# Attention scores of the latent tokens as three float32r products of split operands

## The chip, the cores and the metric

The kernel runs on one core of a Trainium2 chip. The metric is the device time of one execution in microseconds (us); lower is better. TensorE (PE) multiplies, VectorE (DVE) and ScalarE (ACT) do elementwise work and reductions, GpSimd (POOL) and SyncE (SP) mostly issue transfers. Each engine works through its own queue in order and waits at an instruction whose inputs are not there.

## The reference, cut to what matters

One inference step of a two-layer backbone (DEPTH 2) with D_MODEL 1024: 128 context tokens and 256 latent tokens pass through the same weights. A layer is a half-step feed-forward block, a mixer (short convolution, neighbourhood attention NA, latent attention MLA, three gates), and a second feed-forward block. The change touches the scores of both attentions, which have 8 heads each:

```python
# NA: latent queries against the latent keys of the grid (biased, masked) and the cached context keys
s_loc = jnp.einsum('bhrqd,bhrikd->bhrqik', qg, kg).astype(jnp.float32) * NA_SCALE + bias[None]
...
s_ctx = jnp.einsum('bhrqd,bhpd->bhrqp', qg, k_ctx).astype(jnp.float32) * NA_SCALE
prob = jax.nn.softmax(jnp.concatenate([s_loc, s_ctx], axis=-1), axis=-1).astype(v.dtype)
# MLA: latent queries against 256 latent and 128 cached keys; context queries against context keys
s = jnp.einsum('bhqd,bhkd->bhqk', qi, k).astype(jnp.float32) * scale
p = jax.nn.softmax(s, axis=-1).astype(v.dtype)
```

## The kernel before

All 384 tokens lie along the free axis; features lie on partitions. Every dense weight is streamed from memory in chunks of 128x1024 ("raw"), split on chip into a rounded part and a remainder in float32r ("hi" by ScalarE in line 318, "lo" by VectorE in line 319), and multiplied by activations that are split in the same way: three float32r matmuls for each 128-row block (lines 360 to 362, helper mm3). A dense tile is 8 blocks, so 24 matmuls. The attention values and scores are native float32 matmuls on unsplit operands.

The instructions stand in each queue in the order in which the program writes them (a manual schedule). The mixer's function attention works through the MLA heads 0 to 7 one at a time and then through the NA heads in pairs (8,9), (10,11), (12,13), (14,15). For an MLA head i the loop writes: scores([i]); mla_query(i + 2), which makes a later head's query (VectorE, line 945) and, for even heads, the keys of two heads (two ScalarE copies, lines 950 and 951); FILL[i] dense tiles of the convolution branch, each 24 matmuls, with its VectorE work in lines 822 to 838; for odd i the product values(i - 3) of probabilities and values; and transposed(i - 1), seven TensorE transposes of the previous head's probabilities. FILL is 1 behind heads 0, 1, 2, 4 and 6, and 0 behind heads 3, 5 and 7.

scores itself issues the matmuls (lines 862 and 864: two latent query tiles of 128x384, and the context queries of 128x128), then the softmax: three maxima on VectorE (line 877, for NA line 873 with the bias added), a small scaling (line 878), three exponentials on ScalarE (line 883), a reciprocal and three scalings on VectorE (lines 885 and 890). An NA head has 64 features, so two heads of a pair sit on partitions 0 to 63 and 64 to 127 of one tile, and their matmuls use the two halves of the array's rows (the trace writes 64\*128).

Eight PSUM banks (tile ps) rotate through all of this, and eight SBUF tiles of 128x384 (tile w) through all temporaries.

Of the kernel before, what the change touches and what calls it, by code (L numbers as in the profile page):

```python
# [10 lines left out]
F32R = mybir.dt.float32r  # L11
# [7 lines left out]
P = 128  # L19
# [5 lines left out]
NCTX = 128  # L25
NLAT = 256
TOK = NCTX + NLAT
PAST = 128
# [245 lines left out]
class Weights:  # L274
# [49 lines left out]
    def prepare(self):  # L324

        self.split(self.n // BPC + self.ahead)
# [16 lines left out]
def step_kernel(ctx, tc, xT, cc, wst, cst_d, vec_d, rpb, ck_na, cv_na, ck_kv, ck_r, yd, o_k, o_v, o_ckv, o_kr):  # L343
    nc = tc.nc
# [4 lines left out]
    def ps():  # L349
        return psum.tile([P, 512], F32, tag="ps", name="ps")  # L350

    def wt(n=TOK):
        return base.tile([P, TOK], F32, tag="w", bufs=8, name="w")[:, :n]

    def small(n, dtype=F32):
        return base.tile([P, 16], dtype, tag="small", bufs=16, name="small")[:, :n]

    def mm3(out, w, x, start, stop):

        nc.tensor.matmul(out, w[0], x[0], start=start, stop=False)  # L360
        nc.tensor.matmul(out, w[0], x[1], start=False, stop=False)  # L361
        nc.tensor.matmul(out, w[1], x[0], start=False, stop=stop)  # L362

    def split(hi, lo, full):
        nc.scalar.copy(hi, full)  # L365
        nc.vector.tensor_tensor(lo, full, hi.bitcast(F32), op=ALU.subtract)  # L366
# [217 lines left out]
    def dense_tile(h, n=KD, halfway=None):  # L584

        out = ps()
        for k in range(n):
            if halfway and k == n // 2:
                halfway()
            mm3(out[:, :TOK], W.next(), kt(h, k), k == 0, k == n - 1)  # L590
        return out
# [81 lines left out]
    def mixers(l):  # L673
# [6 lines left out]
        with tc.tile_pool(name=f"att{l}", bufs=1, reuse_waits="tile") as pool:  # L680
            attention(l, h, pool, o_conv, o_na, o_mla)
# [33 lines left out]
    def attention(l, h, pool, o_conv, o_na, o_mla):  # L715

        kna = pool.tile([P, 4, ALLK], F32, tag="A8", bufs=3, name="kna")
        qna = pool.tile([P, 4, TOK], F32, name="qna")
# [9 lines left out]
        def bias(heads):  # L728

            for hd in heads:  # L730
                t = biases[hd] = pool.tile([P, 2, TOK], F32, tag="C3", bufs=2, name="bias")
                nc.gpsimd.memset(t[:, :, NLAT:], 0.0)
                nc.gpsimd.dma_start(out=t[:, :, 0:NLAT], in_=rpb[l, hd])
            for hd in heads:
                for qt in range(2):
                    d = biases[hd][:, qt, 0:NLAT].rearrange("p (r c) -> p r c", r=4)
                    nc.gpsimd.tensor_tensor(d, d, cst[:, C_MASK:C_END].unsqueeze(1).to_broadcast([P, 4, 64]),
                                            op=ALU.add)


        low, rb, b = first_group(l, 1)
# [3 lines left out]
        qs, q2, ks = wt(), wt(), wt()  # L745
# [96 lines left out]

        probs, probsT, queries, mla, na = {}, {}, {}, {}, {}

        def scores(heads):


            near = heads[0] >= 8
            scale = 1.0 if near else MLA_SCALE
            operands, tiles = [], []  # L850
            for i in heads:
                if near:
                    r, j = slice(64 * (i % 2), 64 * (i % 2) + 64), i % 8 // 2
                    operands.append((qna[r, j, :], kna[r, j, :]))
                else:
                    operands.append((queries.pop(i), mla["k"][:, i % 4, :]))
                s = ps(), ps()
                tiles.append((s[0][:, :TOK], s[1][:, :TOK], s[0][:, TOK:]))
            for j in range(3):
                for (q, k), s in zip(operands, tiles):  # L860
                    if j < 2:
                        nc.tensor.matmul(s[j], q[:, NCTX + j * P:NCTX + (j + 1) * P], k[:, NCTX:], start=True, stop=True)  # L862
                    else:
                        nc.tensor.matmul(s[2], q[:, :NCTX], k[:, :NCTX], start=True, stop=True)
            cols = [slice(0, TOK), slice(TOK, 2 * TOK), slice(2 * TOK, 2 * TOK + NCTX)]
            n = 3 * len(heads)
            mx, nm, sm, rs = small(n), small(n), small(n), small(n)
            for a, (i, s) in enumerate(zip(heads, tiles)):
                probs[i] = pool.tile([P, 2 * TOK + NCTX], F32, tag="prob", bufs=2, name="prob")
                for j in range(3):  # L870
                    m = mx[:, 3 * a + j:3 * a + j + 1]
                    if near and j < 2:
                        nc.vector.tensor_tensor_reduce(
                            out=probs[i][:, cols[j]], in0=s[j], in1=biases[i % 8][:, j, :], scale=1.0, scalar=-3.0e38,
                            op0=ALU.add, op1=ALU.max, accum_out=m)
                    else:
                        nc.vector.tensor_reduce(m, s[j], axis=AX.X, op=ALU.max)
            nc.vector.tensor_scalar(nm, mx, -scale, None, op0=ALU.mult)
            for a, (i, s) in enumerate(zip(heads, tiles)):
                for j in range(3):  # L880
                    c = 3 * a + j
                    src = probs[i][:, cols[j]] if near and j < 2 else s[j]
                    nc.scalar.activation(probs[i][:, cols[j]], src, AF.Exp, bias=nm[:, c:c + 1], scale=scale,
                                         accum_out=sm[:, c:c + 1])
            nc.vector.reciprocal(rs, sm)
            for a, i in enumerate(heads):
                for j in range(3):
                    c = 3 * a + j
                    p = probs[i][:, cols[j]]
                    nc.vector.tensor_scalar(p, p, rs[:, c:c + 1], None, op0=ALU.mult)  # L890
                biases.pop(i - 8, None)
# [29 lines left out]
        def mla_values():  # L921
            v = mla["v"] = pool.tile([P, 4, 512], F32, tag="A8", bufs=3, name="vmla")
            wh, wl = W.next(4)
            for i in range(4):
                o = ps()
                xh, xl = ckh[:, i * P:(i + 1) * P], ckl[:, i * P:(i + 1) * P]
                nc.tensor.matmul(o, xh, wh, start=True, stop=False)
                nc.tensor.matmul(o, xl, wh, start=False, stop=False)
                nc.tensor.matmul(o, xh, wl, start=False, stop=True)
                (nc.scalar.copy if i % 2 else nc.vector.tensor_copy)(v[:, i, :], o)  # L930

        def mla_query(hd):


            if hd == 0:
                k = mla["k"] = pool.tile([P, 4, ALLK], F32, tag="A8", bufs=3, name="kmla")

                kr = ps()
                nc.tensor.matmul(kr, cst[0:64, C_PM:C_MASK], R, start=True, stop=True)
                nc.scalar.copy(k[0:64, 0::2, :], kr[0:64, :].unsqueeze(1).to_broadcast([64, 2, ALLK]))  # L940
                nc.scalar.copy(k[64:128, 1::2, :], kr[64:128, :].unsqueeze(1).to_broadcast([64, 2, ALLK]))
            o = dense_tile((cqh, cql), 2)
            q = pool.tile([P, TOK], F32, tag="qmla", bufs=3, name="qmla")
            cs = cst[:, C_CSO:C_CSK] if hd % 2 else cst[:, C_CSE:C_CSO]
            nc.vector.tensor_tensor(q, o[:, :TOK], cs, op=ALU.mult)
            queries[hd] = q
            if hd % 2 == 0:
                o = ps()
                mm3(o, W.next(), (ckh, ckl), True, True)
                nc.scalar.copy(mla["k"][64:128, hd % 4, :], o[64:128, :])  # L950
                nc.scalar.copy(mla["k"][0:64, hd % 4 + 1, :], o[0:64, :])

        mla_values()
        mla_query(0)
        mla_query(1)
        for i in range(8):
            scores([i])
            if i + 2 < 8:
                mla_query(i + 2)
            if i == 6:  # L960
                bias([0, 1])
            for _ in range(FILL[i]):
                next(conv)
            if i >= 3 and i % 2:
                values(i - 3)
            if i >= 1:
                transposed(i - 1)
        for i in range(8, 18, 2):
            if i > 8:
                transposed(i - 2)  # L970
                transposed(i - 1)
            if i < 16:
                scores([i, i + 1])
                if i < 14:
                    bias([i - 6, i - 5])
            if i == 8:
                transposed(7)
                na_values()
            for _ in range(FILL[i]):
                next(conv)  # L980
            values(i - 2)
# [64 lines left out]
```

## Time and profile before

| what | value |
|---|---|
| time, median of 3 runs | 1907.8 us (1905.85 to 1907.82) |
| time of the profiled execution | 1906.98 us |
| its span, first to last instruction | 1904.9 us |
| TensorE matmul busy | 1878.2 us, 99% |
| TensorE weight loads busy | 1822.4 us, 96% |
| VectorE busy | 1309.2 us, 69% |
| ScalarE busy | 808.2 us, 42% |
| mean granted TensorE clock | 0.997 of 2.4 GHz |
| heads' scores of layer 0, on TensorE | from 372.9 us; the last of MLA's 8 heads starts at 421.2 us |

Between the span and the time of the execution lie 2.1 us. Matmuls are pipelined: the record of one lasts longer than the distance to the next, so a matmul's price is read from start to start. A native float32 matmul shows as two records, so "x4" in a row of line 862 is two matmuls.

### The profile page before, as it was taken

The numbers are of one execution on the slowest core, as the hardware profiler recorded it, in microseconds if no ns is written. First come the engines' busy times: TensorE is split into PE (matmuls) and PEld (weight loads), VectorE is DVE, ScalarE is ACT, GpSimd is POOL, SyncE is SP. The second block draws the span as 40 slices with busy tenths as digits, with TensorE's granted clock in tenths as the row PEclk, the third lists the DMA queues.
The fourth block names the chain that finished last, engine by engine and source line by source line (L and its number), as shares of the span: only waits on it lengthen the run. The fifth ranks groups of instructions, "written<-read, shape, count | busy, mean of one in ns | idle before, by whom it ended". The sixth has DMA issues, their size and how long they took to land.

```text
span 1904.9 us, 27714 instructions
## 1 busy us (share of the span) xinstructions
PE 1878.2 (99%) x10804; PEld 1822.4 (96%) x10804; DVE 1309.2 (69%) x2235; ACT 808.2 (42%) x1358; POOL 45.0 (2%) x79
## 2 busy tenths in 40 slices
PE   7999999999999999999999999999999999999998
PEld 5999999988999999999999999998789999999998
DVE  6788767665877778776678777676668766744433
ACT  3633334755533454333354333356554334633332
POOL 0000000013000000000000000000220000000000
PEclk9999999999999999999999999999999999999999
DMA  8576655323465535665545665543335543333331
GB/s 305 188 241 223 192 182 162 122 78 112 135 196 184 181 111 188 193 199 190 171 135 191 195 208 180 170 134 118 100 100 176 192 163 122 114 131 123 131 122 67
DMA packets 85523, 306.12 MB, mean 161 GB/s; under 512 B 9616, under 2 KB 11248, under 8 KB 85264
## 3 DMA queue, kind: packets, MB, share of 16 engines
q1 hardware_dynamic: 83376, 297.21, 47.5%
q0 software_dynamic: 1728, 5.41, 1.0%
q8 instruction: 84, 1.38, 0.3%
q10 hardware_dynamic: 288, 1.74, 0.2%
q14 instruction: 47, 0.39, 0.1%
HBM read 301.53 MB, written 2.79 MB: 160 GB/s over the span
## 4 chain that ended last, share of the span: by engine, by line
PE 87%; DVE 6%; ACT 4%; issue 2%; DMA 1%; SPq 0%; DVEq 0%; ACTq 0%
PE ps L361 27%; PE ps L362 27%; PE ps L360 27%; ACT w L525 2%; PE ps L862 1%; PE ps L899 1%; ACT hi L318 1%; DMA raw<-wst 1%; PE ps L915 1%; DVE lo L319 1%; PE ps L808 1%; PE ps L806 1%; PE ps L807 1%; DVE w L433 1%; DVE w L434 1%
## 5 line engine op out<-in xcount | busy, mean ns | idle before, releaser
L361 PE MATMUL ps<-hl,hi 128*128 128x384 f32 (+1 forms) x2176 | 738.4, 339 | 3.1 <-DVE hl L366 2.1
L360 PE MATMUL ps<-hh,hi 128*128 128x384 f32 (+1 forms) x2176 | 735.0, 338 | 3.0 <-ACT hh L365 1.5
L362 PE MATMUL ps<-hh,lo 128*128 128x384 f32 (+1 forms) x2176 | 737.3, 339 | 0.5 <-DVE lo L319 0.5
L319 DVE TENSOR_TENSOR lo<-raw,hi 128x1024 fp32r<-128x1024 f32 x414 | 503.6, 1223 | 226.6 <-ACT hi L318 225.2
L318 ACT CAST hi<-raw 128x1024 fp32r<-128x1024 f32 x414 | 431.0, 1047 | 410.8 <-PE ps L361 268.3
L360 PEld LDWEIGHTS ps<-hh,hi 128*128 128x128 f32 x2176 | 411.1, 189 | 8.4 <-ACT hh L365 4.2
L361 PEld LDWEIGHTS ps<-hl,hi 128*128 128x128 f32 x2176 | 409.6, 188 | 7.0 <-DVE hl L366 5.2
L362 PEld LDWEIGHTS ps<-hh,lo 128*128 128x128 f32 x2176 | 411.3, 189 | 0.9 <-DVE lo L319 0.9
L422 DVE SCALAR_TENSOR_TENSOR junk<-rawa,cb 128x1024 bf16<-128x1024 f32 x256 | 312.8, 1222 | 4.4
L360 PE MATMUL ps<-ah,hi 128*128 128x384 f32 x704 | 237.8, 338 | 0.0
L362 PE MATMUL ps<-ah,lo 128*128 128x384 f32 x704 | 237.8, 338 | 0.0
L361 PE MATMUL ps<-al,hi 128*128 128x384 f32 x704 | 237.8, 338 | 0.0
L365 ACT CAST ah<-w 128x384 fp32r<-128x384 f32 x88 | 45.1, 513 | 273.6 <-DVE w L637 267.0
L360 PEld LDWEIGHTS ps<-ah,hi 128*128 128x128 f32 x704 | 132.2, 188 | 0.0
L361 PEld LDWEIGHTS ps<-al,hi 128*128 128x128 f32 x704 | 132.2, 188 | 0.0
L362 PEld LDWEIGHTS ps<-ah,lo 128*128 128x128 f32 x704 | 132.2, 188 | 0.0
L637 DVE TENSOR_TENSOR w<-w,ps 128x384 f32<-128x384 f32 x76 | 42.0, 552 | 83.3 <-PE ps L362 83.3
L366 DVE TENSOR_TENSOR al<-w,ah 128x384 fp32r<-128x384 f32 x88 | 49.2, 559 | 51.0 <-ACT ah L365 51.0
L599 DVE SCALAR_TENSOR_TENSOR X<-ps,G,X 128x128 f32<-128x128 f32 x96 | 35.6, 412 | 48.6 <-PE ps L362 48.6
L361 PE MATMUL ps<-ol,hi 128*128 128x384 f32 x192 | 64.9, 338 | 0.0
L360 PE MATMUL ps<-oh,hi 128*128 128x384 f32 x192 | 64.8, 338 | 0.0
L362 PE MATMUL ps<-oh,lo 128*128 128x384 f32 x192 | 64.8, 338 | 0.0
(187 smaller groups left out, 1577.3 us busy)
## 6 DMA issues: line engine op xcount, KB each, us to landing
raw<-wst SPq DMA_DIRECT2D x414, 512.0 KB, 3.8
rawa<-wst SPq DMA_DIRECT2D x128, 512.0 KB, 3.4
s<-wst SPq DMA_DIRECT2D x16, 512.0 KB, 9.8
bias<-rpb POOLq DMA_DIRECT2D x16, 256.0 KB, 3.2
X<-xT SPq DMA_DIRECT2D x4, 384.0 KB, 9.5
y<-X SPq DMA_DIRECT2D x3, 512.0 KB, 3.4
cb<-cc ACTq DMA_DIRECT2D x1, 1024.0 KB, 4.6
cst<-cst ACTq DMA_DIRECT2D x1, 672.0 KB, 4.8
```

Source lines behind the costliest of these rows:

```text
L318: nc.scalar.copy(hi, raw)
L319: nc.vector.tensor_tensor(lo, raw, hi.bitcast(F32), op=ALU.subtract)
L360: nc.tensor.matmul(out, w[0], x[0], start=start, stop=False)
L361: nc.tensor.matmul(out, w[0], x[1], start=False, stop=False)
L362: nc.tensor.matmul(out, w[1], x[0], start=False, stop=stop)
L365: nc.scalar.copy(hi, full)
L366: nc.vector.tensor_tensor(lo, full, hi.bitcast(F32), op=ALU.subtract)
L422: nc.vector.scalar_tensor_tensor(junk, w, 1.0, cb[:, v], op0=ALU.mult, op1=ALU.mult, accum_out=mods[l][:, m, t, v:v + 1])
L433: nc.vector.tensor_tensor(a, y, y, op=ALU.mult)
L525: nc.scalar.activation(h[:, sl], h[:, sl], AF.Identity, bias=mods[l][:, 3 * idx, t, s:s + 1], scale=A[0][:, t, s:s + 1])
L599: nc.vector.scalar_tensor_tensor(X[:, t, sl], out[:, sl], g[:, t, s:s + 1], X[:, t, sl], op0=ALU.mult, op1=ALU.add)
L637: nc.vector.tensor_tensor(p, s, u[:, :TOK], op=ALU.mult)
```

## The change

The latent part of the scores becomes a sum of three float32r products of split queries and keys, and the context part stays native. A new function prepare splits a head's (or a pair's) query (256 latent columns) and keys (384 columns) into four w tiles, with the same helper split that the kernel uses elsewhere: a cast on ScalarE (line 365) and a subtraction on VectorE (line 366), each once for the query and once for the keys. prepare for the next head is written behind mla_query(i + 2), so in the queues it stands behind the softmax of head i.

```diff
+        def prepare(heads):
+            i = heads[0]
+            if i >= 8:
+                q, k = qna[:, i % 8 // 2, :], kna[:, i % 8 // 2, :]
+                rows = [slice(64 * e, 64 * e + 64) for e in range(2)]
+            else:
+                q, k = queries.pop(i), mla["k"][:, i % 4, :]
+                rows = [slice(0, P)]
+            qs, ks = [[wt(n).bitcast(F32R) for _ in range(2)] for n in (NLAT, NLAT + PAST)]
+            split(*qs, q[:, NCTX:])
+            split(*ks, k[:, NCTX:])
+            ready[i] = [(q[r], k[r], [x[r] for x in qs], [x[r] for x in ks]) for r in rows]
...
-            for j in range(3):
-                for (q, k), s in zip(operands, tiles):
-                    if j < 2:
-                        nc.tensor.matmul(s[j], q[:, NCTX + j * P:NCTX + (j + 1) * P], k[:, NCTX:], start=True, stop=True)
-                    else:
-                        nc.tensor.matmul(s[2], q[:, :NCTX], k[:, :NCTX], start=True, stop=True)
+            for j in range(2):
+                for n, (a, b) in enumerate(((0, 0), (1, 0), (0, 1))):
+                    for (_, _, q, k), s in zip(operands, tiles):
+                        nc.tensor.matmul(s[j], q[a][:, j * P:(j + 1) * P], k[b], start=n == 0, stop=n == 2)
+            for (q, k, _, _), s in zip(operands, tiles):
+                nc.tensor.matmul(s[2], q[:, :NCTX], k[:, :NCTX], start=True, stop=True)
...
         mla_values()
         mla_query(0)
+        prepare([0])
         mla_query(1)
         for i in range(8):
             scores([i])
             if i + 2 < 8:
                 mla_query(i + 2)
+            prepare([i + 1] if i < 7 else [8, 9])
...
             if i < 16:
                 scores([i, i + 1])
                 if i < 14:
+                    prepare([i + 2, i + 3])
                     bias([i - 6, i - 5])
```

In TensorE's queue, between the scores of MLA heads 3 and 4 of the first layer, there stood before (probT are the transposed probabilities, vmla the values, prob the probabilities, kmla and qmla keys and queries, cqh and cql the split input of the next query):

```order
L362 MATMUL ps<-cqh,lo 128x384
L915 MATMUL ps<-probT,vmla 64x256 x6
L918 MATMUL ps<-probT,vmla 64x128 x2
L899 MATMUL ps<-cst,prob 128x128 x7
L862 MATMUL ps<-kmla,qmla 128x384 x2
L864 MATMUL ps<-kmla,qmla 128x128
```

and there stands now:

```order
L362 MATMUL ps<-cqh,lo 128x384
L927 MATMUL ps<-probT,vmla 64x256 x6
L930 MATMUL ps<-probT,vmla 64x128 x2
L911 MATMUL ps<-cst,prob 128x128 x7
L874 MATMUL ps<-w 128x384 x6
L876 MATMUL ps<-kmla,qmla 128x128
```

The place of the scores has not moved: two matmuls that read kmla and qmla have become six that read the split tiles w.

In VectorE's queue, from the maxima of head 3 to the maxima of head 4 in the first layer, there stood before:

```order
L877 TENSOR_REDUCE small<-ps 128x1 x3
L878 TENSOR_SCALAR small<-small 128x3
L885 RECIPROCAL small<-small 128x3
L890 TENSOR_SCALAR prob<-prob,small 128x384 x2
L890 TENSOR_SCALAR prob<-prob,small 128x128
L945 TENSOR_TENSOR qmla<-ps,cst 128x384
L919 COPY o_mla<-ps 128x384
L877 TENSOR_REDUCE small<-ps 128x1 x3
```

and there stands now:

```order
L889 TENSOR_REDUCE small<-ps 128x1 x3
L890 TENSOR_SCALAR small<-small 128x3
L897 RECIPROCAL small<-small 128x3
L902 TENSOR_SCALAR prob<-prob,small 128x384 x2
L902 TENSOR_SCALAR prob<-prob,small 128x128
L957 TENSOR_TENSOR qmla<-ps,cst 128x384
L366 TENSOR_TENSOR w<-qmla,w 128x256
L366 TENSOR_TENSOR w<-kmla,w 128x384
L931 COPY o_mla<-ps 128x384
L889 TENSOR_REDUCE small<-ps 128x1 x3
```

The two remainders for head 4 stand behind the whole softmax of head 3 and behind the query of head 5. Line numbers behind the new function are 12 higher.

## Rows read from the trace of the kernel before

**Rows 1.** The page's first part: span, and each engine's busy time and share.

```profile
span 1904.9 us, 27714 instructions
PE 1878.2 (99%) x10804; PEld 1822.4 (96%) x10804; DVE 1309.2 (69%) x2235; ACT 808.2 (42%) x1358; POOL 45.0 (2%) x79
```

**Rows 2.** TensorE's waits in the whole span: us, times, longest.

```profile
PE ps L862 <- ACT prob L883: 1.4, 2, 0.7
```

**Rows 3.** TensorE's timeline, a dense tile, then scores of heads 1 and 4: start, us.

```profile
376.14 0.34 PE L360 MATMUL ps<-hh,hi 128*128 128x384 f32 x1
...
380.35 1.45 PE L862 MATMUL ps<-kmla,qmla 128*128 128x384 f32 x4
...
401.29 1.46 PE L862 MATMUL ps<-kmla,qmla 128*128 128x384 f32 x4
402.58 0.39 PE L864 MATMUL ps<-kmla,qmla 128*128 128x128 f32 x2
```

**Rows 4.** VectorE's timeline, softmax of head 3 up to head 4's maxima.

```profile
398.57 1.21 DVE L877 TENSOR_REDUCE small<-ps 128x1 f32<-128x384 f32 x3
...
401.64 0.18 DVE L885 RECIPROCAL small<-small 128x3 f32<-128x3 f32 x1 [1.65 <-ACT prob L883]
401.85 0.94 DVE L890 TENSOR_SCALAR prob<-prob,small 128x384 f32<-128x384 f32 x3
402.71 0.55 DVE L945 TENSOR_TENSOR qmla<-ps,cst 128x384 f32<-128x384 f32 x1
403.18 0.55 DVE L919 COPY o_mla<-ps 128x384 f32<-128x384 f32 x1
403.64 1.21 DVE L877 TENSOR_REDUCE small<-ps 128x1 f32<-128x384 f32 x3
```

**Rows 5.** ScalarE's timeline, the exponentials of head 3, first and last of six.

```profile
400.03 0.58 ACT L883 ACTIVATE prob<-ps,small 128x384 f32<-128x384 f32 x1 [2.23 <-DVE small L878]
...
401.40 0.20 ACT L883 ACTIVATION_READ_ACCUMULATOR prob<-ps,small 128x1 f32 x1
```

**Rows 6.** Splits of other tiles, ScalarE's casts and VectorE's remainders, 128 and 384 columns.

```profile
361.53 0.30 ACT L365 CAST ckh<-ckc 128x128 fp32r<-128x128 f32 x1
363.27 0.51 ACT L365 CAST ckh<-w 128x384 fp32r<-128x384 f32 x1 [1.44 <-DVE w L784]
...
362.43 0.28 DVE L366 TENSOR_TENSOR ckl<-ckc,ckh 128x128 fp32r<-128x128 f32 x1
...
364.68 1.02 DVE L366 TENSOR_TENSOR cql<-w,cqh 128x384 fp32r<-128x384 f32 x2
```

**Rows 7.** VectorE's timeline ahead of the maxima of head 7.

```profile
420.72 1.22 DVE L319 TENSOR_TENSOR lo<-raw,hi 128x1024 fp32r<-128x1024 f32 x1
...
424.79 1.21 DVE L877 TENSOR_REDUCE small<-ps 128x1 f32<-128x384 f32 x3
```

**Rows 8.** ScalarE's key copies and cast ahead of head 0's softmax.

```profile
372.62 0.58 ACT L951 COPY kmla<-ps 64x512 f32<-64x512 f32 x1
373.10 1.04 ACT L318 CAST hi<-raw 128x1024 fp32r<-128x1024 f32 x1
```

**Rows 9.** TensorE's timeline at the pairs (8,9) and (12,13).

```profile
428.63 0.96 PE L899 MATMUL ps<-cst,prob 128*128 128x128 f32 x7
...
461.55 1.75 PE L899 MATMUL ps<-cst,prob 128*128 128x128 f32 x14
463.23 1.56 PE L862 MATMUL ps<-kna,qna 64*128 64x384 f32 x8
464.62 0.39 PE L864 MATMUL ps<-kna,qna 64*128 64x128 f32 x4
```

**Rows 10.** TensorE's timeline early in the kernel, around its first waits.

```profile
13.89 0.44 PE L360 MATMUL ps<-hh,hi 128*128 128x386 f32 x1 [1.37 <-ACT hh L514]
15.19 0.69 PE L361 MATMUL ps<-hl,hi 128*128 128x386 f32 x1 [0.85 <-DVE hl L516]
```

**Rows 11.** Busy times by stretch: us, PE, PEld, DVE, ACT, POOL, granted clock, DMA share, GB/s.

```profile
15.00:20.00 5.00, 4.82 (x25) 4.48 (x29) 2.48 (x5) 1.29 (x2) 0.00 (x0) 0.68 1.03 409
```

More of the change, by code (lines that the diff above doesn't have):

```diff
@@ L843, in attention @@
         probs, probsT, queries, mla, na = {}, {}, {}, {}, {}
+        ready = {}
+        def prepare(heads):
[10 more added lines that the diff above has]
+            ready[i] = [(q[r], k[r], [x[r] for x in qs], [x[r] for x in ks]) for r in rows]
         def scores(heads):
@@ L849, in scores @@
             scale = 1.0 if near else MLA_SCALE
-            operands, tiles = [], []
+            operands, tiles = ready.pop(heads[0]), []
             for i in heads:
-                if near:
-                    r, j = slice(64 * (i % 2), 64 * (i % 2) + 64), i % 8 // 2
-                    operands.append((qna[r, j, :], kna[r, j, :]))
-                else:
-                    operands.append((queries.pop(i), mla["k"][:, i % 4, :]))
                 s = ps(), ps()
                 tiles.append((s[0][:, :TOK], s[1][:, :TOK], s[0][:, TOK:]))
-            for j in range(3):
-                for (q, k), s in zip(operands, tiles):
-                    if j < 2:
-                        nc.tensor.matmul(s[j], q[:, NCTX + j * P:NCTX + (j + 1) * P], k[:, NCTX:], start=True, stop=True)
-                    else:
-                        nc.tensor.matmul(s[2], q[:, :NCTX], k[:, :NCTX], start=True, stop=True)
+            for j in range(2):
[4 more added lines that the diff above has]
+                nc.tensor.matmul(s[2], q[:, :NCTX], k[:, :NCTX], start=True, stop=True)
             cols = [slice(0, TOK), slice(TOK, 2 * TOK), slice(2 * TOK, 2 * TOK + NCTX)]
```

## The prediction

> **What bounds the kernel now.** I read the page's busy times first. TensorE is busy for 1878.2 of 1904.9 us and VectorE for 1309.2 [rows 1], so only what shortens TensorE's queue, or makes TensorE wait, moves the end. Then I read TensorE's waits. In both attentions of both layers it waits at the scores twice, 1.4 us together [rows 2]: once a layer, at the pair (8,9), for a PSUM bank. So each us that TensorE newly waits in the attention is a us at the end, and each us that the products save counts too. The reader is to see why it doesn't wait today. The scores of head i + 1 need only a query and keys that were made a head or two earlier, and nothing of the softmax of head i. The softmax may therefore lag: head 3's maxima start at 398.57 and head 4's at 403.64, while head 4's products have run since 401.29 [rows 3, 4].
>
> **What it removes.** Two native latent products of an MLA head take 402.58 - 401.29 = 1.29 us [rows 3]. A float32r product of the same width costs (380.35 - 376.14) / 24 = 0.175 us, since a dense tile of 24 stands between these two rows. Six are 1.05 us, so TensorE saves 0.24 us for each of 16 heads, 3.8 us in all.
>
> For a pair of NA heads the four native products take 464.62 - 463.23 = 1.39 us [rows 9]. That is little more than two of them would take one after the other, so the two row halves work side by side. The trace has no float32r product on half the rows. If the halves stay side by side, 12 products cost 6 x 0.175 = 1.05 us; one after the other they cost 2.10. Between lies a bound by weight loads: 14 transposes, each with its load, take 463.23 - 461.55 = 1.68 us, 0.12 each, and 12 such would be 1.44. The same two halves in the native rows are the nearest row, so I take 1.25: nearer to side by side, with something for the loads. That saves 0.14 us a pair, with bounds of 0.34 saved and 0.71 lost.
>
> The Trainium skill, TensorEngine Tiling (Array Packing), Key Properties, says that row tiles are independent and can load and multiply in parallel. By that rule a pair would cost 1.05 us and the forecast would be 1.6 us lower. The native rows agree; no run here shows it for float32r.
>
> **What it adds.** Twelve prepares a layer (eight heads, four pairs). A cast takes 0.30 us at 128 columns and 0.51 at 384, a remainder 0.28, and two of 384 in a row 1.02 [rows 6]. For 256 columns I take the middle, 0.41 and 0.42. Back to back, each loses about 0.09 of its record, so a prepare occupies ScalarE for 0.75 us and VectorE for 0.80. Neither engine is the bound, so this alone would cost nothing. What costs is its place.
>
> **The wait it adds.** prepare for head i + 1 stands behind the softmax of head i on both engines, and the products of head i + 1 now wait for it. I follow it from the start of head i's maxima, with the offsets of head 3 [rows 4, 5]. The exponentials begin at 400.03, 1.46 us on, and end at 401.40 + 0.20 = 401.60, 3.03 on. The scalings begin at 3.28, the query of a later head at 4.14, and VectorE is free at 403.18, 4.61 on. Now come the two remainders, so the keys' remainder lands at 4.61 + 0.33 + 0.56 = 5.50. (The casts end at 3.03 + 0.84 = 3.87; two key copies of 0.58 ahead of them [rows 8], behind even heads, only bring them level.) Behind it TensorE still has four of the six products, 0.70, the context scores, 0.21, and some 0.2 until the maxima may read them. So from maxima to maxima at least 5.50 + 1.14 = 6.64 us go by, where 403.64 - 398.57 = 5.07 went by before.
>
> Queued behind the waiting product on TensorE are those of the later heads and all dense tiles; nothing overtakes it. Per layer:
> Head 0: two casts stand ahead of a weight cast that started at 373.10 [rows 8], and the maxima wait for its remainder. +0.75.
> Heads without a fill, 3 to 4 and 5 to 6: 6.64 - 5.07 = 1.57 each. +3.14.
> Heads with a fill (behind 0, 1, 2, 4, 6): TensorE has 4.2 us more of its own, but VectorE has the convolution and weight remainders too. Ahead of head 7's maxima it works without a gap, 424.79 - 420.72 = 4.07 us [rows 7], and two remainders more lengthen that by 0.80. Bounds: 0, if gaps elsewhere take it all, and 0.80. I take 0.65, since the rows are nearer to a full queue. +3.3.
> Head 7 to the pair (8,9): before, 428.63 - 424.79 = 3.84 us from head 7's maxima to the transposes behind the pair [rows 7, 9]. Now there is no later query on the way, so the keys' remainder lands at 5.03, and the rest of the pair's products and contexts takes 1.05 to 1.2. That is 6.15. +2.3.
> The three later pairs: a dense tile or more lies between, and their prepares end 0.8 us behind the scalings for which the 1.68 us of transposes ahead of the scores wait anyway. No wait; 3 x 0.14 saved. -0.4.
> Sum 9.1 a layer, 18.2 for two. The 3.8 us saved on MLA are inside, since the distances are counted with the new products.
>
> **The clock.** Ahead of the pair (8,9) TensorE would idle long: some 3 us until VectorE reaches the maxima (its 4.07 us of other work [rows 7], less the rest of the products, 1.1), then 3.87 to the end of the casts, less the transposes and values that stand between, an estimated 2.7 (seven transposes at 0.12 and eight products of values): about 4.2 us. Early in this trace TensorE idled 1.37 and 0.85 us with one matmul between [rows 10], and the next 5 us ran at a mean granted clock of 0.68 [rows 11]: 1.2 instead of 2.4 GHz for 0.64 of it, 3.2 us, which cost 1.6 us of work. I put 1.2 us a layer here, since part of such a slow stretch would be waited anyway. Bounds: 0, and three falls a layer at 1.6, 9.6 in all.
>
> Total: 18.2 + 2.4 = 20.6 us on the profiled execution's 1906.98, so 1927.6. The median of the runs shown lies 0.8 higher: 1928. My own range for this case is 1921 to 1935.
>
> **The rivals.**
> Only the heads without a fill wait. VectorE's gaps swallow the rest, and five heads save their 0.24. Then 0.75 + 3.14 + 2.3 - 1.2 - 0.4 = 4.6 a layer and no fall of the clock: 9.2, and 1917. For it: VectorE is busy for only 69% of the span [rows 1]. Against: the full queue ahead of head 7 [rows 7].
> The halves don't work side by side in float32r, and the clock falls at other waits too. Eight pairs at 0.85 more than I took are 6.8, the clock up to 7: 1935 to 1942. For it: the slow stretch at so short an idle time [rows 10, 11]. Against: the native pairs [rows 9].
> Not slower: the splits are ready in time. Then only the savings are left, 3.8 + 8 x 0.14 = 4.9: 1903. It decides at the heads without a fill: the keys' remainder would have to land within about 4 us of the maxima instead of 5.50. Against it stand the queues, in which the remainders come behind the scalings.
> That float32r here isn't the faster form I excluded, since the dense tiles use it at 0.175 [rows 3].
>
> **How the numbers follow.** A measurement of this kernel can tell about 0.2%, 3.8 us. Chances: my forecast 0.68; only unfilled heads wait 0.12; halves or clock worse 0.12; not slower 0.05; something between, within 0.2%, 0.03. Faster 0.05, same 0.03, slower 0.92. The range reaches from the forecast's own into the rival on either side, 1916 to 1938. It leaves out the not-slower case (0.05), the one within 0.2% (0.03), a third of the first rival (0.04) and half of the second (0.06), 0.18 in all.
>
> **What would show it.** TensorE's waits must list line 874 waiting for VectorE's line 366 and ScalarE's line 365, some 13 us a layer before the savings, the longest, over 4 us, at the pair (8,9), and none at the three later pairs. From maxima to maxima behind heads 3 and 5: 6.6 us. Six products in 1.05 us where nothing waits. A granted clock below 1 just behind the pair (8,9). I am wrong if the remainders land before TensorE reaches the scores, if the lag doesn't grow behind filled heads, or if a pair's 12 products take 2.1 us.

## The result and the profile after

The changed kernel takes 1931.12 us (median of 4 runs, 1928.86 to 1932.6); the kernel before, beside it on the same chip, takes 1906.91 (1905.85 to 1907.82). The ratio is 1.0126, with a 95% interval of 1.0113 to 1.0139: slower by 24.2 us. The profiled execution took 1930.17 us, 23.2 more than that of before.

The first lines of the page after, to be set beside [rows 1]:

```profile
span 1928.4 us, 27923 instructions
PE 1884.9 (98%) x10868; PEld 1833.5 (95%) x10868; DVE 1329.3 (69%) x2283; ACT 825.4 (43%) x1406; POOL 46.1 (2%) x79
```

VectorE and ScalarE have 20 and 17 us more to do in all, and their shares hardly moved. TensorE should have less to do, and is busy for 6.7 us more: it works for some of the time at half clock. TensorE's waits in the whole span (us in total, times, longest), where [rows 2] had 1.4:

```profile
PE ps L874 <- ACT w L365: 14.2, 9, 3.9
PE ps L874 <- DVE w L366: 4.1, 6, 1.3
```

The score products now wait 18.3 us for casts and remainders, 10.3 of it in the first layer. VectorE's timeline from head 3's maxima to head 4's answers to [rows 4]:

```profile
401.70 1.21 DVE L889 TENSOR_REDUCE small<-ps 128x1 f32<-128x384 f32 x3
...
404.77 0.18 DVE L897 RECIPROCAL small<-small 128x3 f32<-128x3 f32 x1 [1.65 <-ACT prob L895]
404.98 0.94 DVE L902 TENSOR_SCALAR prob<-prob,small 128x384 f32<-128x384 f32 x3
405.84 0.55 DVE L957 TENSOR_TENSOR qmla<-ps,cst 128x384 f32<-128x384 f32 x1
406.31 0.42 DVE L366 TENSOR_TENSOR w<-qmla,w 128x256 fp32r<-128x256 f32 x1
406.64 0.55 DVE L366 TENSOR_TENSOR w<-kmla,w 128x384 fp32r<-128x384 f32 x1
407.11 0.55 DVE L931 COPY o_mla<-ps 128x384 f32<-128x384 f32 x1
408.47 1.02 DVE L889 TENSOR_REDUCE small<-ps 128x1 f32<-128x384 f32 x2 [0.81 <-PE ps L876]
```

(The last row counts two of three maxima, because the view ends at 409.) From maxima to maxima 408.47 - 401.70 = 6.77 us go by instead of 5.07: two remainders, and then 0.81 of waiting for products that had waited for them. The keys' remainder lands at 406.64 + 0.55 = 407.19, 5.49 us behind head 3's maxima. The prepare of the next head stands between the softmax of one head and that of the next, and still ahead of VectorE's copy.

TensorE's timeline, at the scores of head 2, at the pair (8,9), and at the pair (12,13) (the last answers to [rows 9]):

```profile
389.23 1.30 PE L874 MATMUL ps<-w 128*128 128x384 f32 x6
390.37 0.38 PE L876 MATMUL ps<-kmla,qmla 128*128 128x128 f32 x2
...
437.88 0.44 PE L874 MATMUL ps<-w 64*128 64x384 f32 x2 [3.75 <-ACT w L365]
438.70 2.12 PE L874 MATMUL ps<-w 64*128 64x384 f32 x10 [0.38 <-DVE w L366]
440.62 0.63 PE L876 MATMUL ps<-kna,qna 64*128 64x128 f32 x4
441.18 1.11 PE L911 MATMUL ps<-cst,prob 128*128 128x128 f32 x4
...
462.77 1.32 PE L874 MATMUL ps<-w 64*128 64x384 f32 x12
463.93 0.39 PE L876 MATMUL ps<-kna,qna 64*128 64x128 f32 x4
```

Where nothing waits, six products take 1.14 us and a pair's twelve 1.16. At the pair (8,9) TensorE stands still for 3.75 us, and what follows runs slowly. Stretches around that point (granted clock in the last column but two):

```profile
436.00:439.00 3.00, 0.74 (x4) 0.37 (x4) 1.81 (x6) 2.69 (x10) 0.00 (x0) 1.00 0.00 0
440.00:442.50 2.50, 2.50 (x16) 2.28 (x13) 1.12 (x5) 0.00 (x0) 0.01 (x1) 0.50 0.00 0
442.50:445.00 2.50, 2.50 (x14) 2.06 (x13) 1.55 (x7) 0.55 (x2) 1.89 (x4) 0.98 0.33 72
```

A clock of 0.50 is 1.2 GHz; it came behind the idle stretch and lasted some 3 us here, longer in the second layer (0.60 on average from 1379 to 1386). A second fall lies in each layer: at head 6 in the first (0.50 from 423 to 425) and at head 3 in the second (0.50 from 1344 to 1347).

Where the 23.2 us came from is read by setting the starts of the maxima of both profiles beside each other, each counted from its layer's first product of the MLA values. A plain table of what each step adds, in us:

| step | predicted | first layer | second layer |
|---|---|---|---|
| head 0 | 0.75 | 0.71 | 0.72 |
| heads 1, 2, 3, 5, 7 (behind a filled head) | 3.3 | 3.28 | 3.19 |
| head 4 (behind 3, no fill) | 1.57 | 1.70 | 1.71 |
| head 6 (behind 5, no fill) | 1.57 | **3.47** | 1.65 |
| head 7 to the transposes behind the pair (8,9) | 2.3 | 3.25 | 3.24 |
| from there to the last pair's transposes | -0.4 | -0.06 | 0.33 |
| clock, where not in the rows above | 1.2 | | |
| sum | 10.3 | 12.35 | 10.84 |

### The profile page after: what moved, and what is told of

The parts are those of the page before. It is cut to its first block, busy times and chain, and to the rows that moved or that the text cites. A ratio compares the mean times of both kernels' runs of the same rounds, so it can differ in the third digit from the quotient of the medians.

```text
span 1928.4 us, 27923 instructions
## 1 busy us (share of the span) xinstructions
PE 1884.9 (98%) x10868; PEld 1833.5 (95%) x10868; DVE 1329.3 (69%) x2283; ACT 825.4 (43%) x1406; POOL 46.1 (2%) x79
```

## The experiments

Two theories were set against each other. **Place**, the prediction's own: the products wait because their splits stand behind the previous head's softmax; the work itself is free. **Work**: VectorE and ScalarE already set the pace from softmax to softmax, and 0.8 us more a head lengthens that chain, whoever waits for the result.

### Splits early, splits unread, either attention alone

e1_early moves the prepares (and puts half of the queries' splits in two idle tiles):

```diff
         prepare([0])
         mla_query(1)
+        prepare([1])
...
-            prepare([i + 1] if i < 7 else [8, 9])
+            if i < 7:
+                prepare([i + 2] if i < 6 else [8, 9])
```

> The change with each MLA head's splits made one head earlier (those of heads 0 and 1 ahead of the loop, of head i + 2 behind scores of head i, of the pair (8, 9) behind head 6). The same operations, none left out; only their place on VectorE and ScalarE moves. Theory 'place' (the prediction's: the products wait because their splits stand behind the previous head's softmax): the split operands lie ready a head ahead, so the waits of the score products for remainders and casts (18.3 us with the change) go, and what is left is the saving on TensorE, some 16 x 0.16 + 8 x 0.23 = 4.4 us: 1903 to 1908 us. Theory 'work' (VectorE and ScalarE already nearly set the pace of the heads without a dense tile, and 0.8 us more on them for each head lengthens that chain wherever it stands): the products don't wait for splits any more, but the transposes, the values and the PSUM buffers behind them do, and the time stays near that of the change: 1924 to 1932 us.

e2_work_no_wait adds the prepares to the kernel before and lets nothing read them:

```diff
         mla_query(0)
+        prepare([0])
...
+            prepare([i + 1] if i < 7 else [8, 9])
...
+                    prepare([i + 2, i + 3])
```

> The kernel before with its native products, and the casts and remainders of the change computed at the change's places, but read by nothing. Nothing of the reference's computation is left out. Theory 'place': no product waits for a split, and VectorE (67% busy) and ScalarE (41%) have room: 1906 to 1910 us. Theory 'work': the softmax of each unfilled head ends later by the splits ahead of it, and the waits appear at the values (transposed probabilities) and at the PSUM buffers of the pair (8, 9): by a replay of the queues with the rows' durations 4.9 us a layer, 1915 to 1920 us, with no wait of a score product for a remainder.

e3_mla_only and e4_na_only take the new products for one attention:

```diff
# e3_mla_only: native products where near; in prepare
+            if i >= 8:
+                ready[i] = [(q[r], k[r], None, None) for r in rows]
+                return
# e4_na_only: the same with i < 8
```

> The change for the eight MLA heads of a layer alone; the pairs of the neighbourhood attention keep their native products and have no prepare. Theory 'place': each of the MLA heads' own waits stays (18.3 - 2 x 3.9 = 10.5 us), the long one at the pair (8, 9) goes, and 16 x 0.16 = 2.6 us are saved: about 1915 us (1912 to 1918). Theory 'work': what the eight splits put on VectorE and ScalarE has already delayed the softmax of head 7, so the pair's successors wait as long for it without a prepare of their own: 7.5 us a layer by the same replay, 1920 to 1926 us.

> The change for the four pairs of the neighbourhood attention alone; the MLA heads keep their native products. Theory 'place': the splits of the pair (8, 9) stand behind the softmax of head 7 as with the change, so its 3.75 to 3.94 us of waiting stay, less 8 x 0.23 = 1.8 us for the products: about 1912.5 us (1910 to 1915). Theory 'work': that wait is so long only because seven splits have delayed head 7; alone it takes the place of the pair's other waits, some 1.9 - 0.7 = 1.2 us a layer more: 1907 to 1911 us.

Measured, with 1906.66 us for the kernel before: e1_early 1925.26 (ratio 1.0100, 1.0083 to 1.0117), e2_work_no_wait 1919.65 (1.0067, 1.0052 to 1.0082), e3_mla_only 1923.10 (1.0084, 1.0069 to 1.0099), e4_na_only 1913.67 (1.0038, 1.0025 to 1.0051).

e1_early lies in the range of "work". Splits that nothing reads cost 13.0 us, again the range of "work". That ends the claim that the work alone is free. VectorE's timeline in e2_work_no_wait, from head 3's maxima to head 4's:

```profile
402.09 1.22 DVE L887 TENSOR_REDUCE small<-ps 128x1 f32<-128x384 f32 x3
...
406.69 0.42 DVE L366 TENSOR_TENSOR w<-qmla,w 128x256 fp32r<-128x256 f32 x1
407.03 0.55 DVE L366 TENSOR_TENSOR w<-kmla,w 128x384 fp32r<-128x384 f32 x1
407.50 0.55 DVE L929 COPY o_mla<-ps 128x384 f32<-128x384 f32 x1
407.96 1.21 DVE L887 TENSOR_REDUCE small<-ps 128x1 f32<-128x384 f32 x3
```

The distance is 5.87 instead of 5.07: two remainders longer, with VectorE never idle for a product. The lag is then collected by TensorE further on, at the pair's PSUM bank (line 872) and at the values (line 925). Its waits at these lines in the whole span, e2_work_no_wait first:

```profile
PE ps L872 <- ACT prob L893: 4.0, 2, 2.0
PE ps L925 <- ACT probT L910: 3.5, 4, 1.4
```

These waits are 7.5 us, where [rows 2] had 1.4. They don't show all of the lag, since the modelled ends of the matmul records reach into the idle time: counted from each layer's start, the last transposes come 6.3 and 5.2 us later than before (in the first layer the clock fell at the pair as well). The change costs 11.2 us more than e2_work_no_wait, although its products are shorter. So the waiting of the products, with the falls of the clock behind it, has a price of its own on top of the work: behind head 3 it is 6.77 us from maxima to maxima with the change and 5.87 without the waits.

The same waits in e1_early (values at line 931, scores at line 878):

```profile
PE ps L931 <- ACT probT L916: 9.9, 5, 2.4
PE ps L878 <- ACT prob L899: 6.5, 4, 2.6
...
PE ps L878 <- ACT w L365: 1.9, 2, 0.9
```

In e1_early the products wait for splits for 1.9 us instead of 18.3, and TensorE's waits in the attention come to 18.3 us all the same. A head earlier was also a bad place: the remainders there stand right behind the making of the query that they split, so VectorE waits for its own cast too:

```profile
409.32 0.43 DVE L366 TENSOR_TENSOR sql<-qmla,sqh 128x256 fp32r<-128x256 f32 x1 [0.47 <-ACT sqh L365]
```

ScalarE waits there as well, 13.6 us in 8 casts that stand ahead of exponentials and weight casts and need a query that VectorE has yet to make. So e1_early changes two things at once: the products' waiting goes, and new waits come on both engines. Alone it doesn't decide between the theories; e2_work_no_wait and e12_in_gaps below do.

The two attentions add up: e3_mla_only's 16.4 us and e4_na_only's 7.0 make 23.4 of the 24.2. For MLA "work" was right (its 1920 to 1926 holds 1923.1). For the pairs "place" was (1910 to 1915 holds 1913.67): alone they cost 7.0 us, through the wait that "place" named. TensorE's waits in e4_na_only:

```profile
PE ps L880 <- ACT w L365: 6.1, 2, 3.1
...
PE ps L880 <- DVE w L366: 0.8, 2, 0.4
```

and the stretches behind the wait in the first layer, with the clock at 0.50 for 5 us:

```profile
425.00:430.00 5.00, 1.79 (x10) 1.35 (x12) 2.81 (x10) 3.15 (x10) 0.00 (x0) 0.83 0.01 2
430.00:435.00 5.00, 5.00 (x23) 4.29 (x20) 2.67 (x11) 0.49 (x1) 1.85 (x4) 0.50 0.10 35
```

### The pair's splits early; fills moved; casts alone

```diff
# e5_na_early, on e4_na_only
-            prepare([i + 1] if i < 7 else [8, 9])
+            if i < 7:
+                prepare([i + 1])
+            if i == 1:
+                prepare([8, 9])
# e6_fill_after on the change, e7_fill_before on the kernel before
-FILL = {0: 1, 1: 1, 2: 1, 3: 0, 4: 1, 5: 0, 6: 1, 7: 0, 8: 0, 10: 2, 12: 2, 14: 2, 16: 1}
+FILL = {0: 1, 1: 1, 2: 1, 3: 1, 4: 1, 5: 1, 6: 1, 7: 1, 8: 0, 10: 1, 12: 1, 14: 1, 16: 1}
# e8_casts, on e2_work_no_wait
-            split(*qs, q[:, NCTX:])
-            split(*ks, k[:, NCTX:])
+            nc.scalar.copy(qs[0], q[:, NCTX:])
+            nc.scalar.copy(ks[0], k[:, NCTX:])
```

> The split products for the neighbourhood attention alone, with the splits of the pair (8, 9) made behind head 1's scores instead of behind head 7's, where heads 0 to 2 have a dense tile each; its later pairs as in the change. Nothing is left out. Theory 'the pair waits for its place' (with the pair's splits behind head 7 it cost 7 us where 8 x 0.23 = 1.9 us should have been saved): the wait of 3.0 + 0.4 us a layer and the clock's fall behind it go, and the saving shows: 1903.5 to 1906 us. Theory 'work': the 1.55 us of splits lengthen the heads of the loop wherever they stand, and the pair comes later by as much: 1907 to 1911 us.

> The change, with three dense tiles a layer moved from the later pairs to the MLA heads 3, 5 and 7, so that every MLA head has one and each later pair one. The same work, in another order; to be compared with the kernel before in the same order, e7_fill_before. Theory 'work, and it decides at the unfilled heads': a dense tile covers VectorE and ScalarE, and the difference to e7_fill_before is that of the first heads less the products' saving, about 1 us a layer: 0 to +5 us, and no wait of a product above 2 us behind heads 4 to 7. By the prediction's own term for filled heads (+0.65 each) it is 7 x 0.65 + 0.75 - 1.2 = 4.1 us a layer: about +8 us. Theory that each head pays for the splits whatever covers them: near the +24 us of the change.

> The kernel before, with the same three dense tiles a layer moved to the heads 3, 5 and 7: the partner of e6_fill_after. Nothing is left out. If the pairs of the neighbourhood attention keep enough cover with one dense tile each, it is 1903 to 1908 us (the pair (8, 9)'s wait of 0.6 to 0.8 us may go); if they were covered by the second tile, the wait moves to them: 1910 to 1920 us.

> As e2_work_no_wait (the native products of the kernel before, splits read by nothing), with ScalarE's casts alone: the remainders on VectorE are not computed. Nothing of the reference's computation is left out. It divides the 13 us of e2_work_no_wait between the two engines. If VectorE's 0.80 us a head are what lengthens the chain, the casts alone cost 0 to 4 us (1907 to 1911 us); if ScalarE's 0.75 us, which stand ahead of the transposed probabilities' copies and the next head's exponentials, do: 1914 to 1920 us.

Measured, with 1906.52 us for the kernel before: e5_na_early 1905.40 (0.9996, 0.9987 to 1.0005), e6_fill_after 1921.46 (1.0076, 1.0063 to 1.0090), e7_fill_before 1912.28 (1.0033, 1.0021 to 1.0045), e8_casts 1913.51 (1.0035, 1.0021 to 1.0049).

e5_na_early: one call moved brings 1913.67 down to 1905.40, within "the pair waits for its place". The waits for splits are gone, and what is left is the PSUM wait that the kernel before had too:

```profile
PE ps L880 <- ACT prob L901: 2.4, 2, 1.3
```

Each later pair is 0.24 us shorter, but the time is not measurably better than before's: in the first layer the last pair's transposes come 0.8 us earlier, counted from the layer's start, since at the pair (8,9) the PSUM wait takes the saving. The pair's splits behind head 1 are work on the chain too: head 2's maxima come 0.80 us later. Head 5's come 0.79 closer to head 4's than before, so the lag is gone before TensorE has to wait for it.

e6_fill_after against e7_fill_before: 9.2 us, not 24.2, and not the 0 to 5 of "work" either. It lies nearest the prediction's term for filled heads, +8. The maxima say where. From e7_fill_before to e6_fill_after the first layer's heads 0 to 3 add 0.72, 0.74, 0.80 and 0.72 us, heads 4 to 7 add -0.1, 0.7, 0.6 and -0.2, and the rest up to the last transposes nothing. So a dense tile doesn't cover the splits at heads 1 to 3, where the change's own profile had shown 0.73 to 0.80 each as well, and behind them it does so at some heads only. I had no theory for this difference beforehand, and why heads 4 and 7 are covered stays open. The last transposes come 3.9 us later in the first layer and 3.1 in the second, each counted from its layer's start; another 1.2 us between the two profiles lie ahead of the first layer's attention, where the two kernels are the same. Moving the tiles is no gain by itself: e7_fill_before is 5.8 us slower than the kernel before, since transposes now wait for scalings.

e8_casts: 7.0 us, between its two ranges. The casts alone cost about half of the 13.0. That the remainders cost the other half is the difference of two runs and wasn't measured by itself; but VectorE can't be all of the chain.

### GpSimd

```diff
# e9_pool_rem, on e1_early
-            split(*qs, q[:, NCTX:])
-            split(*ks, k[:, NCTX:])
+            for (hi, lo), x in ((qs, q), (ks, k)):
+                nc.scalar.copy(hi, x[:, NCTX:])
+                nc.gpsimd.tensor_tensor(lo, x[:, NCTX:], hi.bitcast(F32), op=ALU.subtract)
# e10_pool_all: nc.gpsimd.tensor_copy in place of nc.scalar.copy
# e11_no_mask, on the change
-            for hd in heads:
+            for hd in heads if heads[0] else []:
                 for qt in range(2):
```

> e1_early (splits a head earlier) with the remainders computed by GpSimd instead of VectorE; the casts stay on ScalarE. The same values. Theory 'the work on the two engines of the softmax costs, not the waiting for splits': with VectorE's share gone, what is left is about that of e8_casts, 7.0 us, less the products' 4.4 us saving: 1907 to 1911 us. Rival 'GpSimd's elementwise work slows VectorE while it runs' (two remainders of head 6 took 0.82 and 1.08 us instead of 0.42 and 0.55 beside GpSimd's mask additions): GpSimd works some 1.75 us a prepare (its additions of 256 columns take 0.7 each), and VectorE loses up to as much again as it was relieved of: 1916 to 1926 us, with VectorE's maxima, scalings or weight remainders longer than in the kernel before.

> e1_early with casts and remainders both on GpSimd (four of its instructions a prepare, an estimated 3.5 us from its additions' 0.7 us for 256 columns). The same values. Theory 'work': neither VectorE nor ScalarE has more to do than before, so only the saving is left if GpSimd keeps up and disturbs nobody: 1902 to 1905 us. Rival 'GpSimd slows VectorE': VectorE is slowed for twice as long as in e9_pool_rem, and the time is above that kernel's; waits of the score products for GpSimd's remainders may come on top in the unfilled heads (5 us each, against 3.5 us of GpSimd's work).

> The change without the additions of the mask to the biases of the first pair, heads 0 and 1 of the neighbourhood attention (that part of the computation is left out, four GpSimd instructions a layer). If these additions were what stretched head 6's two remainders in the first layer (0.82 and 1.08 us instead of 0.42 and 0.55), the remainders are back at 0.42 and 0.55, the maxima of head 7 follow those of head 6's predecessor as in the second layer (8.61 us becomes 6.8), and the time falls by 1 to 2 us: 1929 to 1930.5 us. If the additions had nothing to do with it, remainders and time stay: 1931 us.

Measured, with 1906.89 us for the kernel before: e9_pool_rem 1928.48 (1.0114, 1.0099 to 1.0129), e10_pool_all 1916.77 (1.0050, 1.0035 to 1.0065), e11_no_mask 1929.14 (1.0117, 1.0100 to 1.0134).

e9_pool_rem is slower than e1_early. Both GpSimd kernels leave VectorE the 2235 instructions of the kernel before, and its busy time on their pages is 1325.6 and 1325.5 us, against 1309.2 before and 1332.6 in e1_early: the same instructions took 16 us longer, so of some 23 us of remainders VectorE was relieved of only 7. The rival's mechanism is in the VectorE timeline of e9_pool_rem at head 6:

```profile
427.07 0.18 DVE L902 RECIPROCAL small<-small 128x3 f32<-128x3 f32 x1 [1.66 <-ACT prob L900]
427.28 2.41 DVE L907 TENSOR_SCALAR prob<-prob,small 128x384 f32<-128x384 f32 x3
```

and GpSimd's in the same stretch:

```profile
427.46 0.83 POOL L864 TENSOR_TENSOR w<-qna,w 128x256 fp32r<-128x256 f32 x1 [2.08 <-PE ps L916]
428.26 1.10 POOL L864 TENSOR_TENSOR w<-kna,w 128x384 fp32r<-128x384 f32 x1
```

Three scalings that take 0.94 us in [rows 4] took 2.41 while GpSimd subtracted. e10_pool_all was expected above e9_pool_rem by the rival and at 1902 to 1905 by "work"; it is at neither. It takes all splits off both engines of the softmax, is the faster of the two by 11.7 us, and still loses 9.9, with scalings of 2.31 and 1.87 us in its heads. So "work" holds in direction. The rest goes with VectorE's longer instructions and with products that wait for GpSimd (2.3 us in e10_pool_all, 1.0 in e9_pool_rem); how much each has isn't separated. Nor is the contention shown to be all of e9_pool_rem's loss: over heads 0 to 3 of its first layer the maxima fall back by 6.7 us, with scalings of 0.94 to 0.95, and e1_early fell back by 6.1 there.

e11_no_mask settles the 3.47 us at head 6. VectorE's remainders there, in the first layer of the change, with GpSimd's additions:

```profile
420.90 3.27 POOL L737 TENSOR_TENSOR bias<-bias,cst 128x256 f32<-128x256 f32 x4 [1.30 <-DMA bias<-rpb]
```

```profile
421.08 0.82 DVE L366 TENSOR_TENSOR w<-qmla,w 128x256 fp32r<-128x256 f32 x1
421.82 1.08 DVE L366 TENSOR_TENSOR w<-kmla,w 128x384 fp32r<-128x384 f32 x1
```

and without the additions, in e11_no_mask:

```profile
420.39 0.42 DVE L366 TENSOR_TENSOR w<-qmla,w 128x256 fp32r<-128x256 f32 x1
420.72 0.56 DVE L366 TENSOR_TENSOR w<-kmla,w 128x384 fp32r<-128x384 f32 x1
```

The distance from head 5's maxima to head 6's went from 8.61 to 6.78 us there, as expected. The medians differ by 2.0 us, in different sets of runs and with overlapping intervals, so the time alone would not show it. In the second layer a fall of the clock came at another place than in the change (0.76 from 1350 to 1355) and cost about 1.5 us at heads 4 and 5: of the 1.4 us that the first layer won, the second gave back 1.1.

### The splits inside the previous head's softmax

```diff
# e12_in_gaps, on the change
-        def scores(heads):
+        def scores(heads, following=None):
...
             nc.vector.tensor_scalar(nm, mx, -scale, None, op0=ALU.mult)
+            if following:
+                prepare(following)
...
-            prepare([i + 1] if i < 7 else [8, 9])
```

> The change with each prepare issued inside the previous head's softmax: its casts stand ahead of that head's exponentials on ScalarE, where ScalarE waits 2.2 to 2.7 us for the maxima, and its remainders between the negated maxima and the reciprocal on VectorE, where VectorE waits 1.65 us for the exponentials. The same operations, none left out; head 0's own prepare stays where the change has it. Refined theory 'a place on the chain of the softmax': work is paid where VectorE or ScalarE is what the next head waits for, and free in these two gaps, so the maxima follow each other as in the kernel before (5.07 us behind heads 3 and 5), and what is left is the saving of 4.4 us less 0.72 us a layer at head 0: 1902.5 to 1905.5 us, the fastest of all. Theory 'work, wherever it stands' (12.7 to 13 us for splits that nothing reads, 23 us for splits a head early): 13 - 4.4 us over the kernel before, 1913 to 1918 us.

Measured, with 1906.80 us for the kernel before: 1908.43 (median of 11 runs; 1.0008, 0.9999 to 1.0017). Of the change's 24.2 us, 22.6 are gone, with the same instructions on every engine. VectorE's timeline, from head 3's maxima to head 4's, to be set beside the same stretch of the change above:

```profile
399.38 1.21 DVE L889 TENSOR_REDUCE small<-ps 128x1 f32<-128x384 f32 x3
400.63 0.17 DVE L890 TENSOR_SCALAR small<-small 128x3 f32<-128x3 f32 x1
400.71 0.42 DVE L366 TENSOR_TENSOR w<-qmla,w 128x256 fp32r<-128x256 f32 x1
401.04 0.55 DVE L366 TENSOR_TENSOR w<-kmla,w 128x384 fp32r<-128x384 f32 x1
402.44 0.18 DVE L899 RECIPROCAL small<-small 128x3 f32<-128x3 f32 x1 [0.86 <-ACT prob L897]
...
404.45 1.21 DVE L889 TENSOR_REDUCE small<-ps 128x1 f32<-128x384 f32 x3
```

The remainders lie in the time in which VectorE waits for the exponentials: 0.86 us of waiting is left of 1.65, and from maxima to maxima it is 5.07 us again. But the time stayed 3 us above the expected range, and the 4.4 us that the products should save don't show. Two places are left. Head 0's own prepare still costs 0.7 us a layer. And the pair (8,9) still waits; TensorE's waits there:

```profile
PE ps L874 <- DVE w L366: 2.2, 2, 1.2
```

Its splits stand in head 7's softmax, which comes late. In the first layer the clock fell to 0.50 behind that wait (427 to 429); from the pair's transposes to the next ones it is 19.98 us there and 19.21 in the second layer, where it didn't fall. Counted from the layer's start, the last pair's transposes come 0.93 us later than before in the first layer and 0.75 earlier in the second. One gap was not empty: ScalarE's load of a table, 1.28 us, ran ahead of head 0's exponentials while they waited for the maxima, and now stands behind the new casts; head 1's maxima come 0.82 us later, head 5's take it back, and no product waits for it. The profiled execution, 1906.09 us, is one of the fastest of the 11; what the median has on top of it no profile shows, and it stays open. This kernel with the pair's splits of e5_na_early was not tried; it might take that wait away.

## Why the prediction was right, and where not

**Direction and size.** 1928 was forecast, 1931.1 measured. The terms for head 0, for the five filled heads and for head 4 were met within 0.15 us in both layers, so the chain from maxima to maxima was counted rightly: the keys' remainder was to land 5.50 us behind the maxima and landed at 5.49; 6.64 to the next maxima were forecast, 6.77 and 6.78 measured behind head 3, 6.79 behind head 5 in the second layer. The term for the filled heads fits its sum better than its parts, and that is luck: 0.65 was taken for each, and heads 1 to 3 added 0.73 to 0.81, head 5 only 0.40. The shortfall of 3 us is made of the misses below.

**The sentence that failed.** "Neither engine is the bound, so this alone would cost nothing. What costs is its place." The first half is wrong as written: unread splits cost 13.0 us. The terms of the sum had it right without saying so, since 0.65 for a filled head is the price of two remainders on VectorE. The second half stands in a sharper form: what counts first is a place on the chain from softmax to softmax or in one of its gaps (e12_in_gaps); the waiting of the products comes on top (6.77 against 5.87 us behind head 3).

**MLA products.** 0.24 us a head was too much: the six take 1.14 us, not 1.05, and save 0.15 to 0.17.

**NA pairs.** 1.16 us where 1.25 was taken. The halves work side by side in float32r, nearer to the 1.05 that followed from the Trainium skill, TensorEngine Tiling (Array Packing), Key Properties. A pair saves 0.23 to 0.24 us, and the three later pairs wait for nothing, as forecast.

**Head 6 in the first layer.** The one large miss, 1.9 us: GpSimd's mask additions stretched the remainders by 0.93 us, and the clock fell behind the longer wait. The prediction counted GpSimd nowhere.

**The pair (8,9).** 2.3 was forecast and 3.25 measured. The keys' remainder landed 5.02 us behind the maxima (5.03 forecast); the 0.94 more is the half clock on the products and context scores, which the prediction had as a term of its own. From the pair's fifth product to what follows its context scores 2.01 us went by, and 1.02 at the pair (12,13). Its 1.2 us a layer came out as 1.6 and 2.0: 0.94 here, and 0.66 and 1.05 up to the last transposes, where three pairs should have saved 0.72.

**The waits.** 13 us a layer were to be listed and 9.2 were; the place and the pair's 3.75 to 3.94 (over 4 forecast) are close. A lag from maxima to maxima is not all idle time of TensorE: part is its own work, at half clock or not.

**The rivals.** That only unfilled heads wait is excluded by 3.2 to 3.3 us a layer at the filled ones, that the halves go one after the other by 1.16. "Not slower, the splits are ready in time" was priced at 1903. e1_early shows that being ready in time is not enough, and e12_in_gaps that the change can come to no measurable difference, though not to the saving.

## What to carry to other kernels

Work added to an engine that is 43% or 69% busy is not free where that engine's chain paces a stage: ask in which of its idle gaps the instructions fall. A chain of two engines that hand over to each other, as a softmax does, has a gap on each in every round. Work put there cost nothing from maxima to maxima at the heads 2 to 4 of e12_in_gaps, while the same work behind the last step of the round cost its whole length. But look at what runs in the gap already. Making a result earlier helps little if its making stays on that chain (18.6 of 24.2 us stayed in e1_early, which brought new waits of its own).

## What the runs showed of the hardware

**GpSimd and VectorE hold each other up.** In the first layer of the change GpSimd's additions began at 420.90, just ahead of VectorE's remainder at 421.08. The remainders were stretched, 0.42 and 0.55 to 0.82 and 1.08, and the additions too, 2.83 in the kernel before to 3.27. In the second layer the remainder began first:

```profile
1364.16 0.42 DVE L366 TENSOR_TENSOR w<-qmla,w 128x256 fp32r<-128x256 f32 x1
1364.50 0.55 DVE L366 TENSOR_TENSOR w<-kmla,w 128x384 fp32r<-128x384 f32 x1
1364.24 3.49 POOL L737 TENSOR_TENSOR bias<-bias,cst 128x256 f32<-128x256 f32 x4 [1.56 <-DMA bias<-rpb]
```

There the remainders were undisturbed, and it was the additions that took longer, 3.49 us instead of 2.83. The Trainium skill, SBUF — State Buffer, Who interferes with whom, says that VectorE and GpSimd share a pair of ports, that a VectorE instruction with two inputs in SBUF contends with a GpSimd instruction that reads SBUF, and that the order of issue decides who blocks. Both layers agree with it.

**A fall of the clock isn't always paid.** In the second layer of the change the fall at head 3 delayed the transposes behind it by 1.55 us against the first layer, and by head 3's own transposes the difference was 0.03: TensorE's waits for head 4's splits were 0.35 us there instead of 1.63, so the slow stretch took the place of waiting. In the second layer of e11_no_mask a fall of the same kind stood one head later and its 1.5 us stayed.
